# Two of layer 1's adaLN groups made in layer 1's own mixers, with staging of their own

## The chip, the cores and the metric

The kernel runs on one core of a Trainium2 chip. The metric is the device time of one execution in microseconds. The kernel before takes 2099.42 us (median of three runs, 2098.45 to 2099.58).

The core has five engines that run their own instruction lists beside each other: TensorE (PE, matrix products and transposes), VectorE (DVE), ScalarE (ACT), GpSimd (POOL), and SyncE (SP), which here issues all loads. PE writes to PSUM, the others read it from there; everything else lives in the on-chip memory SBUF, and weights come from HBM by DMA.

## The reference, cut to what matters

Two layers, a stream of 256 context tokens and 256 latent tokens, width 1024, float32. In the last layer only the latent tokens are updated. Each layer first needs six modulation vectors (adaLN) for each of two conditions, from one wide product:

```
def adaln_params(cond, lp):
    return jnp.split(jax.nn.silu(cond) @ lp['w_ada'] + lp['b_ada'], 6, axis=-1)

def trunk_layer(xc, xl, c, c_ctx, lp, row, col, update_ctx):
    mod_l = [m[:, None, :] for m in adaln_params(c, lp)]
    mod_c = adaln_params(c_ctx, lp)
    hc = modulate(xc, mod_c[0], mod_c[1])
    hl = modulate(xl, mod_l[0], mod_l[1])
    yc, yl = token_mixer(hc, hl, lp, row, col, update_ctx)
    xl = layer_norm(ALPHA * xl + mod_l[2] * yl, lp['ln1_g'], lp['ln1_b'])
    fl = expert_choice_ffn(modulate(xl, mod_l[3], mod_l[4]), lp)
    xl = layer_norm(ALPHA * xl + mod_l[5] * fl, lp['ln2_g'], lp['ln2_b'])
    ...
```

The token mixer has three branches, an S5 state space, a latent attention (MLA) and a windowed attention. Each branch output is projected (w_branch) and multiplied by a sigmoid gate of 1024 columns; then one output projection (w_out) follows. The feed-forward part has 16 experts (w_gate, w_up, w_down: 3 x 4 MB each). Vectors 0 and 1 are needed before the mixers, 2 to 5 only behind them.

## The kernel before

**Stages.** The program goes through layer 0 and then layer 1. In each: layer norm and modulation, projection to the branches' inputs, the S5 main loop, its GLU, the window projections and the window attention, MLA, output projection and router, experts. In the trace S5's loop stands at 135 to 245 us (layer 0) and 1285 to 1376 (layer 1), the experts at 740 to 1200 and 1660 to 2076.

**The S5 loop** (`s5_main`) has eight steps. Step m records `head(m)` (matmuls into "sc", products L842 and L843 on DVE, sums on POOL, eight scans L852), then `tail(m - 1)` (matmuls into "mm", copies on ACT, transposes into "tp"), the tables of the next head (L818 to L825), `turn(m)` (L862, L863 and POOL's L868), and then a tick.

**Fill work.** A tick adds to a debt in the planner's price unit; while there is debt, `step` takes the next piece of a fill generator (`gates`, `branches`, `gated`) and records it there. One gate is one w_in load of 1024x128 (0.5 MB), its split into two rounded parts (L404 on ACT, L407 on DVE or POOL; "wc"), and 24 matmuls into "F". Every piece of fill work also pays into `ada_debt`, and while that is positive, `step` takes the next step of an adaLN group.

**An adaLN group** (`ada_group`) makes two of the six vectors for both conditions: eight steps (k), each with two loads of w_ada of 128x1024 (0.5 MB) and eight matmul instructions into "ad" (two records each in the trace, `ad<-arena,silu_c`), priced 1.6; then its end: the sum with the bias row on DVE (L376), four transposes into "tp", and copies to modT (L384, L386). Of the six groups (layer, number), (0,0) is made at the start, and the five others are queued in layer 0, before its S5 loop. Their loads take turns in the staging ring "stg" with all w_in and w_branch loads.

**Order on the engines.** The code records instructions; a scheduler then orders each engine's list from the dependencies. A slot of a PSUM tag ("tp" has two, "sc" and "mm" two, "F" and "ad" one) goes from one user to the next in the order in which they were recorded, so a later user can't pass an earlier one of the same tag.

**Late columns.** The last 4096 columns of the on-chip arena (`LATE`) are held by a buffer "late" that no instruction uses during the mixers; they are freed for the experts.

Of the kernel before, what the change touches and what calls it, by code (L numbers as in the profile page):

```python
# [157 lines left out]
class Net:  # L158
# [48 lines left out]
    def step(self):  # L207
        try:
            us = next(self.fillq[0])
            self.debt -= us  # L210
            self.ada_debt += us
        except StopIteration:
            self.fillq.pop(0)
        while self.adaq and self.ada_debt > 0:
            try:
                self.ada_debt -= next(self.adaq[0])
            except StopIteration:
                self.adaq.pop(0)
# [132 lines left out]
    def ada_group(self, l, g, bufs=None):  # L351

        nc = self.nc
        R = self.adarow[(l + g) % 2]
        self.load(R, self.ins["b_rep"][l, g])
        pt = self.ps("ad")
        scv = self.sc.rearrange("p (k s) -> p k s", s=32)
        src = self.ins["w_ada"][l, g]
        for k in range(KT):
            if bufs and k < 7:  # L360
                self.load(bufs[k], src[k])
                ws = [bufs[k][:, 0:1024], bufs[k][:, 1024:2048]]
            else:
                ws = []
                for h in range(2):
                    ws.append(self.stg())
                    self.load(ws[h], src[k, :, 1024 * h:1024 * h + 1024])
            for h in range(2):
                for j in range(4):

                    i = self.mm(pt[32 * j:32 * j + 32, 256 * h:256 * h + 256], scv[:, k, :],
                                ws[h][:, 256 * j:256 * j + 256], k == 0 and h == 0, k == KT - 1)
                    if k == 0 and h + j:
                        self.tc.keep_in_program_order(i)
            yield 1.6
        nc.vector.tensor_tensor(R, pt, R, op=OP.add)  # L376
        tp = self.ps("tp")
        for b in range(4):
            self.tr(tp[:, b * 128:(b + 1) * 128], R[:, b * 128:(b + 1) * 128])
        tv = tp.rearrange("p (b jj jm s) -> p jj jm b s", b=4, jj=2, jm=2)  # L380
        for jj in range(2):
            m = 2 * g + jj
            dst = self.modT[l % 2][:, m].rearrange("p (jm b) s -> p jm b s", jm=2)
            self.nc.vector.tensor_copy(dst, tv[:, jj, :, :, 0:2])  # L384
            if m in (1, 4):
                nc.vector.tensor_scalar(self.modT[l % 2][:, m], self.modT[l % 2][:, m], 1.0, None, op0=OP.add)  # L386
        self.adaR[l % 2, g] = True
        yield 0.0

    def mod_row(self, l, m, s, dst, scale=1.0):  # L390
# [1299 lines left out]
    def build(self, layers=(0, 1), stop=None):  # L1690
        tc, nc = self.tc, self.nc
        self.dbg_out = {}
        self.fillq, self.adaq, self.debt, self.ada_debt = [], [], 0.0, 0.0
        with tc.tile_pool(name="main", bufs=1) as main, \
                tc.tile_pool(name="small", bufs=1) as small, \
                tc.tile_pool(name="ps", bufs=1, space=PSUM) as psum:
            self.small, self.psum, self.main = small, psum, main
            self.sc = main.tile([128, KT * 32], F32, name="silu_c")
            self.modT = [main.tile([128, 6, KT, 2], F32, name=f"modT{i}") for i in range(2)]
            k1 = main.tile([128, 4], F32, name="k1")  # L1700
            self.mhalf, self.econst, self.hpi, self.ones1 = [k1[:, i:i + 1] for i in range(4)]
            for ap, val in ((self.mhalf, -0.5), (self.econst, math.e), (self.hpi, math.pi / 2), (self.ones1, 1.0)):
                nc.vector.memset(ap, val)
            self.const = main.tile([128, NCONST], F32, name="const")
            arena = main.tile([128, self.ARENA_COLS], F32, name="arena")
            self.A = Arena(arena, self.ARENA_COLS)
            self.adaR, self.OH, self.ah, self.cd, self.back, self.norm, self.rw, self.rrow = {}, {}, {}, {}, {}, {}, {}, {}
            self.buf("late", 4096, at=self.LATE)
            self.adarow = [self.buf(f"ada{i}", 512, low=True) for i in range(2)]
            x = {t: self.buf(f"x{t}", D, low=True) for t in range(4)}  # L1710
            self.ada_start()
            self.load(self.const[:, 0:128], self.ins["const"][:, 0:128])
            self.S, self.early, self.stats, self.T, self.feed = {}, [], {}, {}, lambda: None
            self.setup = self.s5_setup(layers[0], self.S, 16)
            next(self.setup)
            self.stg = self.rot("stg", 1024, 4, True)
            hb = [self.block(f"h{i}", F32) for i in range(2)]
            bufs = [hb[i // 2][:, 2048 * (i % 2):2048 * (i % 2) + 2048] for i in range(4)]
            bufs += [self.block(f"extra{i}", F32)[:, 0:2048] for i in range(2)] + [self.buf("wada", 2048, True)]
            for k, _ in enumerate(self.ada_group(layers[0], 0, bufs)):  # L1720
                if k == 4:
                    for t in range(4):
                        self.load(x[t], self.xin(t))
                if k in (7, 8):
                    kc = len(self.early)
                    self.early.append(self.wload(self.w_in(layers[0], 0, 512)[:, 2 * kc:2 * kc + 2], 2, 512))
            self.free("wada")
            for l in layers:
                self.layer(l, x, 1 if l == 0 and 1 in layers else None)
            for t in (2, 3):  # L1730
                self.load(self.out[0, (t - 2) * 128:(t - 1) * 128], x[t])

    def xin(self, t):
        return self.ins["ctx" if t < 2 else "x"][0, (t % 2) * 128:(t % 2) * 128 + 128]

    def layer(self, l, x, nxt):
        tc, nc = self.tc, self.nc
        full = l == 0
        q0 = 0 if full else 256
        N = 512 - q0  # L1740
        with tc.tile_pool(name=f"parts{l}", bufs=1, reuse_waits="tile") as self.R:
            if l:
                self.stg = self.rot("stg", 1024, 3, at=20288)
            step, pts = self.s5_product(l)
            if (l % 2, 1) not in self.adaR:
                self.load(self.const[:, 128:], self.ins["const"][:, 128:])
            h = self.modulated_split(l, x, [full or t < 2 for t in range(4)], step, self.stats)
            self.free(*[f"x{t}" for t in range(4 if full else 2)])
# [2 lines left out]
                pass  # L1751
            S = self.S
            Z = self.proj_tok(l, h, full)
            if (l % 2, 1) not in self.adaR:
                self.adaq += [self.ada_group(l, 1), self.ada_group(l, 2)]
            if nxt is not None:
                self.adaq += [self.ada_group(nxt, g) for g in range(3)]
            mT = self.buf("mT", KT * N, True, 12416 if full else None).rearrange("p (k n) -> p k n", k=KT)
            self.fill(self.gates(l, h, 0, mT, q0))
            if not full:  # L1760
# [78 lines left out]
        with tc.tile_pool(name=f"late{l}", bufs=1, reuse_waits="tile") as pool:  # L1839
            NS = 2 if full else 1  # L1840
            xs = pool.tile([128, 2048 * NS], F32, name="xs")
            XS = xs.rearrange("p (g k e c) -> p g k e c", g=2, k=KT, e=4)
            XS = [XS[:, g] for g in range(2)]
            grow(blocks=[] if full else [(pool.tile([128, 2048], F32, name="more"), 192)],
                 single=[xs[:, 2048:]] if full else [])
            self.free(*[f"m2{s}" for s in m2])
            grow(*T["F2"])
            AFF = self.buf("raff", 64 * NS, at=T["raff"]).rearrange("p (t s e) -> p t s e", t=2, s=NS)
            nc.gpsimd.memset(AFF, 0.0)
            for s in ((1, 0) if full else (1,)):  # L1850
                self.out_norm(l, pts[s], x, s, gb)
                if s == 2 - NS:
                    self.free("lngb")
                    grow(*T["F3"])
                tags = ("sc", "sc", "F", "ad") if NS == 1 or not s else ("tp", "tp")
                self.scores(l, s, x, s + NS - 2, AFF, tags)
            self.free(*[f"x{t}" for t in tts])
            grow(*T["F4"])
            self.choose(l, AFF, NS)
            grow(*T["F5"])  # L1860
            pts = self.moe(l, x, self.xn, full, weight, XS, nxt)
            self.T = {}
            tts = (0, 1, 2, 3) if full else (2, 3)
            self.free(*[n for n in self.A.live if n[0] in "EF"])
            self.buf("late", 4096, at=self.LATE)
            self.finish(l, x, pts, nxt is not None)

    ARENA_COLS = 27456
# [86 lines left out]
```

## Time and profile before

| | |
|---|---|
| median of 3 runs | 2099.42 us |
| the profiled execution | 2097.34 us |
| its span | 2095.6 us |
| PE / DVE / ACT / POOL busy | 86% / 50% / 29% / 22% of the span |
| mean granted TensorE clock | 0.917 |
| read from HBM | 541.09 MB |

The span runs from the first to the last instruction of the trace; the 1.7 us between it and the time of that execution lie outside. A busy share is an average over stages with different limits, so a stage has to be read for itself. A wait is written with what ended it ("<-"). In the chain of waits each piece is the work, transfer or wait that the end of the kernel hangs on at that moment.

### The profile page before, as it was taken

To read this page: it belongs to the slowest core of one execution; us is meant where nothing else is said; L and a number is where in the kernel's file an instruction comes from. 1 tells how busy PE (TensorE), PEld (TensorE's weight loads), DVE (VectorE), ACT (ScalarE), POOL (GpSimd) and SP (SyncE) were. 2 spreads that over 40 slices of the span, in tenths; PEclk is the share of its full clock that TensorE was granted. 3 is DMA by queue.
4 is the path that set the end of the run, shared out by engine and by line. 5 is a ranking of instruction groups with operands and counts; after the bars stand their busy time and mean duration, and the time that the engine had idled before them with its cause. 6 is when DMAs were issued, how large, how long until landed. Compare 5 with 4: busy or idle time off the path is not lost.

```text
span 2095.6 us, 31733 instructions
## 1 busy us (share of the span) xinstructions
PE 1791.9 (86%) x12425; PEld 1112.2 (53%) x12425; DVE 1042.9 (50%) x2431; ACT 611.3 (29%) x1353; POOL 451.5 (22%) x590
## 2 busy tenths in 40 slices
PE   5899899999999699999799979799998776676765
PEld 2876666677777544434233368787786532232221
DVE  6767666756528712313555367977767321010102
ACT  2444253344424311101111165654553110000000
POOL 5735320011125100001343034641114000000000
PEclk8999999999999799999999989999999888776777
DMA  9236744522247689999999733342267799999996
GB/s 334 67 123 218 245 144 163 163 78 71 60 132 274 248 354 421 421 421 416 416 413 351 297 91 94 81 129 63 76 214 297 291 420 421 421 421 421 420 421 272
DMA packets 173013, 544.20 MB, mean 260 GB/s; under 512 B 18624, under 2 KB 101696, under 8 KB 122816
## 3 DMA queue, kind: packets, MB, share of 16 engines
q1 hardware_dynamic: 172864, 542.18, 68.2%
q8 instruction: 98, 1.61, 0.3%
q14 instruction: 51, 0.42, 0.1%
HBM read 541.09 MB, written 1.05 MB: 259 GB/s over the span
## 4 chain that ended last, share of the span: by engine, by line
PE 54%; DMA 23%; DVE 14%; POOL 3%; ACT 3%; issue 3%; SPq 0%; POOLq 0%; ACTq 0%; DVEq 0%
PE sc L243 16%; PE mm L243 16%; PE F L243 13%; DMA arena<-in_w_down 4%; DMA arena<-in_w_up 4%; PE tp L246 4%; PE ad L243 4%; DMA arena<-in_w_gate 3%; DVE extra L852 2%; DVE wc L407 2%; DMA h<-in_w_gate 2%; DMA big<-in_w_gate 2%; DMA arena<-in_w_in 1%; DMA extra<-in_w_up 1%; DMA extra<-in_w_gate 1%
## 5 line engine op out<-in xcount | busy, mean ns | idle before, releaser
L243 PE MATMUL F<-h,wc 128*128 128x256 f32 (+1 forms) x1200 | 237.1, 350 | 11.3 <-ACT arena L1295 9.0
L404 ACT ACTIVATE wc<-arena 128x512 fp32r<-128x512 f32 (+2 forms) x280 | 169.9, 619 | 208.6 <-DMA arena<-in_w_in 45.8
L407 DVE TENSOR_TENSOR wc<-arena,wc 128x512 fp32r<-128x512 f32 (+2 forms) x205 | 163.3, 808 | 112.9 <-ACT wc L404 112.5
L243 PE MATMUL sc<-arena,xs 128*32 128x256 f32 (+1 forms) x1336 | 188.5, 522 | 33.7 <-DMA arena<-in_w_up 20.5
L243 PEld LDWEIGHTS F<-h,wc 128*128 128x128 f32 x1200 | 188.5, 196 | 42.6 <-ACT arena L1295 9.9
L243 PE MATMUL mm<-arena 128*32 128x256 f32 (+5 forms) x1244 | 186.1, 467 | 21.9 <-DMA arena<-in_w_down 13.4
L246 PE MATMUL tp<-const,arena 128*128 128x128 f32 (+2 forms) x819 | 137.5, 293 | 70.4 <-DVE arena L1618 11.6
L1641 DVE TENSOR_TENSOR arena<-mm,arena 32x512 f32<-32x512 f32 (+1 forms) x128 | 70.9, 554 | 219.0 <-PE mm L243 217.4
L407 POOL TENSOR_TENSOR wc<-arena,wc 128x512 fp32r<-128x512 f32 (+2 forms) x75 | 96.9, 1292 | 376.3 <-ACT wc L404 316.7
L246 PEld LDWEIGHTS tp<-const,arena 128*128 128x128 f32 (+2 forms) x819 | 97.3, 147 | 130.5 <-issue 38.5
L238 ACT ACTIVATE arena<-tp 128x512 f32<-128x512 f32 (+3 forms) x142 | 61.9, 463 | 341.7 <-PE tp L246 297.4
L260 POOL TENSOR_TENSOR lnq<-lnq,k 128x1 f32<-128x1 f32 x22 | 16.5, 750 | 568.8 <-DVE lnq L307 530.0
L243 PEld LDWEIGHTS sc<-arena,xs 128*32 128x32 f32 (+1 forms) x1336 | 60.8, 131 | 139.7 <-issue 68.7
L243 PEld LDWEIGHTS mm<-arena 128*32 128x32 f32 (+2 forms) x1244 | 76.3, 137 | 107.2 <-issue 50.5
L243 PE MATMUL sc<-h,xs 128*32 128x256 f32 (+1 forms) x752 | 112.3, 533 | 21.0 <-DMA h<-in_w_gate 13.2
L1618 DVE TENSOR_TENSOR arena<-arena,sc 128x512 f32<-128x512 f32 (+1 forms) x32 | 17.7, 554 | 178.2 <-PE sc L243 177.9
L243 PE MATMUL sc<-big,xs 128*32 128x256 f32 (+1 forms) x632 | 80.8, 487 | 25.2 <-DMA big<-in_w_gate 13.0
L1616 ACT ACTIVATE arena<-sc 128x512 f32<-128x512 f32 (+1 forms) x32 | 15.7, 491 | 295.1 <-PE sc L243 295.1
L243 PE MATMUL mm<-wc,h 128*128 128x512 f32 (+2 forms) x288 | 79.1, 399 | 11.3 <-ACT h L496 4.4
L243 PE MATMUL F<-extra,wc 128*128 128x256 f32 (+1 forms) x432 | 85.7, 343 | 3.5 <-DVE arena L1330 3.1
L1617 DVE SCALAR_TENSOR_TENSOR arena<-arena,sc 128x512 f32<-128x512 f32 (+1 forms) x32 | 17.7, 554 | 142.3 <-ACT arena L1616 142.2
L243 PEld LDWEIGHTS sc<-h,xs 128*32 128x32 f32 (+1 forms) x752 | 36.8, 133 | 89.2 <-issue 60.7
(344 smaller groups left out, 3183.1 us busy)
## 6 DMA issues: line engine op xcount, KB each, us to landing
arena<-in_w_up SPq DMA_DIRECT2D x65, 1024.0 KB, 16.8
arena<-in_w_down SPq DMA_DIRECT2D x61, 1024.0 KB, 19.8
arena<-in_w_gate SPq DMA_DIRECT2D x48, 1024.0 KB, 19.7
arena<-in_w_ada SPq DMA_DIRECT2D x82, 512.0 KB, 5.0
h<-in_w_gate SPq DMA_DIRECT2D x41, 1024.0 KB, 15.0
arena<-in_w_in SPq DMA_DIRECT2D x66, 512.0 KB, 4.0
big<-in_w_up SPq DMA_DIRECT2D x26, 1024.0 KB, 19.8
h<-in_w_down SPq DMA_DIRECT2D x26, 1024.0 KB, 18.6
```

What stands on the lines that cost most here:

```text
L238: self.nc.scalar.activation(out, in_, AF.Copy)
L243: return self.nc.tensor.matmul(out, lhsT, rhs, start=start, stop=stop, skip_group_check=True)
L246: self.nc.tensor.transpose(out, in_, self.c("idn")[:n, :n])
L260: self.nc.gpsimd.tensor_tensor(out, in_, e.to_broadcast(list(in_.shape)), op=OP.pow)
L404: nc.scalar.activation(hi, src, AF.Copy)
L407: eng.tensor_tensor(lo, src, hi.bitcast(F32), op=OP.subtract)
L852: v.tensor_tensor_scan(z, rb, z, 0.0, op0=OP.mult, op1=OP.add)
L1616: nc.scalar.activation(th, gu[0][:, :NF], AF.Tanh, scale=0.5)
L1617: v.scalar_tensor_tensor(th, th, 1.0, gu[0][:, :NF], op0=OP.add, op1=OP.mult)
L1618: v.tensor_tensor(th, th, gu[1][:, :NF], op=OP.mult)
L1641: v.tensor_tensor(YS[n][o:o + 32, c * NF:(c + 1) * NF], yp[r:r + 32, :NF], m5[r:r + 32], op=OP.mult)
```

## The change

In layer 0 the queue holds three groups, (0,1), (0,2) and (1,0); (1,1) and (1,2) are queued in layer 1, before its S5 loop. What a piece of fill work pays into `ada_debt` is multiplied by `ADA`, 0.35 in layer 0 and 0.2 in layer 1. The adaLN loads get a ring of their own (`astg`) in the late columns: four buffers in layer 0, three in layer 1, where the two bias rows (`adarow`) take the rest. The record of finished groups (`adaR`) goes, and two conditions with it.

```
@@ step @@
-            self.ada_debt += us
+            self.ada_debt += us * self.ADA
@@ ada_group @@
-                    ws.append(self.stg())
+                    ws.append(self.astg())
...
-        self.adaR[l % 2, g] = True
@@ build @@
-            self.buf("late", 4096, at=self.LATE)
+            self.take_late(4)
...
+    def take_late(self, n):
+
+        late = self.buf("late", 4096, at=self.LATE)
+        bufs = [late[:, i:i + 1024] for i in range(4096 - 1024 * n, 4096, 1024)]
+        if n < 4:
+            self.adarow = [late[:, 0:512], late[:, 512:1024]]
+        at = [0]
+
+        def nxt():
+            at[0] += 1
+            return bufs[(at[0] - 1) % n]
+
+        self.astg = nxt
@@ layer @@
+        self.ADA = 0.35 if full else 0.2
...
-            if (l % 2, 1) not in self.adaR:
+            if full:
                 self.load(self.const[:, 128:], self.ins["const"][:, 128:])
...
-            if (l % 2, 1) not in self.adaR:
-                self.adaq += [self.ada_group(l, 1), self.ada_group(l, 2)]
+            self.adaq += [self.ada_group(l, 1), self.ada_group(l, 2)]
             if nxt is not None:
-                self.adaq += [self.ada_group(nxt, g) for g in range(3)]
+                self.adaq.append(self.ada_group(nxt, 0))
...
-            self.buf("late", 4096, at=self.LATE)
+            self.take_late(3)
             self.finish(l, x, pts, nxt is not None)
```

The lines of DVE's and PE's lists below are one lower in the changed kernel (L842 is L841 there, L407 is L406), because a line above them went.

VectorE in layer 1's S5 loop, kernel before, from the end of head 3 to head 4; `sc_9387` and `sc_9404` are the two PSUM tiles of head 4, `wc` are weight splits:

```order
L852 SCALAR_TENSOR_TENSOR extra_8866<-s5rho,extra_8866 128x128 x2
L862 TENSOR_TENSOR arena<-extra_8866,arena 128x256
L863 TENSOR_TENSOR arena<-extra_8866 128x256
L852 SCALAR_TENSOR_TENSOR extra_8866<-s5rho,extra_8866 128x128 x2
L407 TENSOR_TENSOR wc<-arena,wc 128x512
L862 TENSOR_TENSOR arena<-extra_8866,arena 128x256
L863 TENSOR_TENSOR arena<-extra_8866 128x256
L842 TENSOR_TENSOR arena<-sc_9387,extra_8866 128x512
L843 TENSOR_TENSOR arena<-sc_9387,extra_8865 128x512
L821 TENSOR_SCALAR arena<-extra_8866 128x516
L822 SCALAR_TENSOR_TENSOR arena<-arena,extra_8866 128x516
L842 TENSOR_TENSOR arena<-sc_9404,extra_8866 128x512
```

The same place in the changed kernel; `ad_8868` is the PSUM tile of group (1,2), `tp_8860` and `tp_8950` hold the transposes of the two groups:

```order
L862 TENSOR_TENSOR arena<-extra_8685 128x256
L406 TENSOR_TENSOR wc<-arena,wc 128x512
L820 TENSOR_SCALAR arena<-extra_8685 128x516
L821 SCALAR_TENSOR_TENSOR arena<-arena,extra_8685 128x516
L384 COPY modT_66<-tp_8860 128x16 x2
L406 TENSOR_TENSOR wc<-arena,wc 128x512 x10
L376 TENSOR_TENSOR arena<-ad_8868,arena 128x512
L406 TENSOR_TENSOR wc<-arena,wc 128x512
L384 COPY modT_66<-tp_8950 128x16 x2
L386 TENSOR_SCALAR modT_66<-modT_66 128x16
L406 TENSOR_TENSOR wc<-arena,wc 128x512 x2
L841 TENSOR_TENSOR arena<-sc_9387,extra_8685 128x512
```

Between heads 3 and 4 stand now the last copies of the first group, the whole end of the second and 14 splits; in the kernel before one split stood there.

TensorE behind head 4 in the kernel before: `mm_9421` and `mm_9422` are the tiles of tail 3, `F_9361` is the seventh gate (G6):

```order
L243 MATMUL sc_9404<-arena,big_7003 64x128 x4
L243 MATMUL mm_9421<-arena,big_7002 64x64
L243 MATMUL mm_9422<-arena,big_7002 64x64
L243 MATMUL mm_9421<-extra_8865,big_7001 64x64
L243 MATMUL mm_9422<-extra_8865,big_7001 64x64
```

and in the changed kernel:

```order
L243 MATMUL sc_9404<-arena,big_6822 64x128 x4
L243 MATMUL F_9361<-h_8242,wc 128x256
L243 MATMUL F_9361<-h_8243,wc 128x256
L243 MATMUL F_9361<-h_8242,wc 128x256 x2
L243 MATMUL F_9361<-h_8243,wc 128x256
L243 MATMUL F_9361<-h_8242,wc 128x256 x2
L246 MATMUL tp_8860<-const,arena 128x128 x4
L243 MATMUL ad_8868<-arena,silu_c 32x256 x8
```

From here on the list holds G6 to G14 (nine gates) and the 64 instructions of `ad_8868` between them, in pieces of 4 or 8; behind them come the transposes `tp_8950`, G15 and the first matmul of tail 2.

SyncE in layer 0, from the loads of the last gates on, kernel before; `in_w_in 128x8x128` is one gate's weights or one of the five loads of the window projections:

```order
L229 DMA arena<-in_w_in 128x8x128
L229 DMA arena<-in_w_ada 128x1024 x3
L229 DMA arena<-in_s_w_glu 128x4x512
L229 DMA arena<-in_w_ada 128x1024 x3
L229 DMA arena<-in_b_rep 128x512
L229 DMA arena<-in_w_in 128x8x128 x5
L229 DMA arena<-in_w_branch 128x4x256
```

and in the changed kernel:

```order
L229 DMA arena<-in_w_in 128x8x128
L229 DMA arena<-in_w_ada 128x1024 x2
L229 DMA arena<-in_w_in 128x8x128
L229 DMA arena<-in_s_w_glu 128x4x512
L229 DMA arena<-in_w_ada 128x1024 x3
L229 DMA arena<-in_w_branch 128x4x256
L229 DMA arena<-in_w_ada 128x1024
```

All 13 loads of w_in stand ahead of s_w_glu now, with two w_ada loads between two of them where there were up to six.

## Rows read from the trace of the kernel before

**Rows 1.** The page's head and busy table: engine, busy us (share), instructions.

```profile
span 2095.6 us, 31733 instructions
PE 1791.9 (86%) x12425; PEld 1112.2 (53%) x12425; DVE 1042.9 (50%) x2431; ACT 611.3 (29%) x1353; POOL 451.5 (22%) x590
```

**Rows 2.** Table by stage: stretch, us, busy of PE, PEld, DVE, ACT, POOL, PEclk, DMA, GB/s.

```profile
130.00:260.00 130.00, 114.92 (x1155) 77.65 (x1154) 96.01 (x162) 48.09 (x92) 64.50 (x75) 0.97 0.65 214
...
300.00:420.00 120.00, 117.65 (x773) 79.49 (x772) 79.68 (x244) 46.62 (x134) 8.75 (x8) 0.99 0.48 156
...
1280.00:1376.00 96.00, 76.61 (x871) 70.73 (x872) 88.99 (x151) 57.09 (x106) 64.05 (x77) 0.93 0.37 96
1376.00:1402.00 26.00, 26.00 (x165) 23.21 (x162) 15.84 (x43) 14.86 (x45) 7.70 (x11) 0.93 0.44 131
...
1660.00:2096.00 436.00, 293.95 (x3104) 119.05 (x3096) 63.12 (x148) 23.36 (x56) 1.10 (x2) 0.76 0.97 402
```

**Rows 3.** Chain of waits in layer 0: start us, us, what.

```profile
183.35 3.00 PE ad L243 x32
...
224.24 5.09 PE F L243 x21
...
231.32 4.88 DMA arena<-in_w_ada
...
236.95 5.67 DMA arena<-in_w_in
...
251.64 5.45 DMA arena<-in_w_in
...
402.23 4.03 DMA arena<-in_w_ukvp
```

**Rows 4.** SyncE's queue, layer 0: start us, us, instruction, count.

```profile
144.65 18.24 SPq L229 DMA_DIRECT2D arena<-in_w_ada  x6
162.99 1.64 SPq L229 DMA_DIRECT2D arena<-in_w_in  x1
...
271.14 3.66 SPq L229 DMA_DIRECT2D arena<-in_w_in  x3
```

**Rows 5.** Table by stretch, of the adaLN matmuls (silu_c) alone; last PE, PEld, DVE.

```profile
100.00:245.00 145.00, 24.00 (x328) 8.87 (x328) 0.00 (x0) 0.98 0.56 185
245.00:300.00 55.00, 7.02 (x88) 2.17 (x88) 0.00 (x0) 1.00 0.62 192
300.00:420.00 120.00, 18.26 (x224) 6.35 (x224) 0.00 (x0) 0.99 0.48 156
```

**Rows 6.** VectorE's timeline, layer 0's S5, first and last head: start us, us, instruction.

```profile
135.49 0.69 DVE L842 TENSOR_TENSOR arena<-sc,extra 128x512 f32<-128x512 f32 x1 [1.67 <-PE sc L243]
...
233.69 0.69 DVE L842 TENSOR_TENSOR arena<-sc,arena 128x512 f32<-128x512 f32 x1 [2.13 <-PE sc L243]
```

**Rows 7.** Costliest groups from 130 to 260 us: instruction, count, busy us, mean ns, idle before.

```profile
L243 PE MATMUL mm<-extra,big 64*64 64x128 f32 x256 | 22.9, 276 | 2.0 <-POOL extra L868 2.0
L243 PE MATMUL sc<-arena,big 64*64 64x128 f32 x256 | 17.6, 272 | 0.0
```

**Rows 8.** Chain of waits in layer 1, S5 and behind it.

```profile
1307.32 3.04 PE F L243 x24
...
1375.43 0.91 PE mm L243 x24
1376.34 4.32 PE F L243 x22
...
1382.48 3.04 PE F L243 x24
...
1387.83 1.77 PE F L243 x15
...
1390.46 1.06 PE F L243 x9
```

**Rows 9.** VectorE's timeline, layer 1's S5.

```profile
1296.80 0.40 DVE L862 TENSOR_TENSOR arena<-extra,arena 128x256 f32<-128x256 f32 x1
1297.11 0.41 DVE L863 TENSOR_TENSOR arena<-extra 128x256 f32<-128x256 f32 x1
...
1305.99 2.44 DVE L852 TENSOR_TENSOR_SCAN extra<-s5rho,extra 128x128 f32<-128x128 f32 x4
1308.35 0.40 DVE L862 TENSOR_TENSOR arena<-extra,extra 128x256 f32<-128x256 f32 x1
...
1324.41 0.69 DVE L842 TENSOR_TENSOR arena<-sc,extra 128x512 f32<-128x512 f32 x1 [0.31 <-issue]
1325.02 0.68 DVE L843 TENSOR_TENSOR arena<-sc,extra 128x512 f32<-128x512 f32 x1
```

**Rows 10.** Table by stretches of 20 us, columns as in rows 2.

```profile
240.00:260.00 20.00, 17.27 (x152) 9.96 (x145) 6.95 (x10) 5.10 (x14) 4.99 (x5) 1.00 0.83 279
1300.00:1320.00 20.00, 17.18 (x194) 16.10 (x194) 18.35 (x32) 12.14 (x24) 15.54 (x17) 0.87 0.33 81
...
1620.00:1640.00 20.00, 8.83 (x67) 7.19 (x67) 14.41 (x51) 7.20 (x16) 2.20 (x4) 0.65 0.58 224
...
1660.00:1680.00 20.00, 20.00 (x362) 11.63 (x358) 4.01 (x11) 3.91 (x6) 0.00 (x0) 1.00 1.01 420
```

More of the change, by code (lines that the diff above doesn't have):

```diff
@@ L1706, in build @@
             self.A = Arena(arena, self.ARENA_COLS)
-            self.adaR, self.OH, self.ah, self.cd, self.back, self.norm, self.rw, self.rrow = {}, {}, {}, {}, {}, {}, {}, {}
-            self.buf("late", 4096, at=self.LATE)
+            self.OH, self.ah, self.cd, self.back, self.norm, self.rw, self.rrow = {}, {}, {}, {}, {}, {}, {}
+            self.take_late(4)
             self.adarow = [self.buf(f"ada{i}", 512, low=True) for i in range(2)]
```

## The prediction

> **What bounds the kernel now.** The page's head and busy table come first: TensorE (PE) is busy for 86% of the span, VectorE (DVE) for 50% [rows 1]. Those shares are averages, so the second view is the table by stage [rows 2]. The reader is to see four things in it. From 300 to 420 us PE is busy 117.65 of 120: what PE is spared there comes back as time. From 130 to 260 (layer 0's S5 and what follows) PE has 114.92 of 130 and DVE 96.01: neither is full, and the chain of waits must say who is late. From 1280 to 1376 (layer 1's S5) DVE has 88.99 of 96, PE 76.61: DVE bounds it. From 1660 on the transfers are busy 97% of the time at 402 GB/s: layer 1's experts cost what their bytes cost, and mixers that end later by some time end the kernel later by that time.
>
> Third, the chain through layer 0 [rows 3]. It holds 3.00 us of adaLN matmuls (PE ad, x32), a wait of 4.88 us for a transfer of w_ada, and two for w_in, 5.67 and 5.45 us. The sync queue shows why w_in is late [rows 4]: a single load stands behind six of w_ada (18.24 us for one such six), all through one staging ring, and the first loads of the window projections go out only at 271.14. A last wait, 4.03 us at 402, is for w_ukvp [rows 3]. So the adaLN groups hurt layer 0 today.
>
> **Part 1, what layer 0 is spared.** Two of five groups leave it. The adaLN matmuls by themselves [rows 5] take 24.00 + 7.02 + 18.26 = 49.28 us of PE for 328 + 88 + 224 = 640 records, five groups: 9.9 us each, two are 19.7.
>
> Inside S5: the DVE work of the first of its eight heads begins at 135.49, that of the last at 233.69 [rows 6], so seven steps take 98.2 us, 14.0 each. In PE's order a step has about one gate (24 matmuls; at 5.09 for 21 [rows 3] 5.8 us), one head and one tail (17.6 and 22.9 us over eight, side by side in part [rows 7]: some 4 us) and until now 20 to 24 adaLN instructions (9.9 us over 64, so 3.4): 13.2 together, near the step of now. With 8 such instructions left PE needs 11, and DVE's 96.01/8 = 12.0 at most [rows 2] becomes the limit. I take 1.5 us a step, -11 in all, between -5 (the POOL and ACT waits inside the steps stay) and -14.
>
> Behind S5: w_in no longer queues behind w_ada (sync order in the change section). Of the 5.67 and 5.45 us I take -7, between -3 and -11, because about as many adaLN instructions stay behind S5 as stood there before. The load of w_ukvp now stands ahead of most of w_ada: -3, between 0 and -4. The own staging adds no instruction and no byte. The loads that move before 60 us I cost at nothing, 2 us either way: POOL and DVE carry that stretch. Layer 0: **-21 us**, between -8 and -28.
>
> **Part 2, what layer 1 gets.** "A fifth of the rate" isn't what the code does. The debt that releases adaLN steps is never cleared. Layer 0's fill work is priced by the planner at 40.8 (gates) + 20.8 (branches) + 2 x 61.6 (gated) = 184.8; times 0.35 that is 64.7, and three groups at 8 x 1.6 use up 38.4. So 26.3 are left when layer 1 begins, and its two groups cost 25.6: both are recorded whole at the first tick of S5, behind head 0. (These are the planner's prices, not times.) The transposes' two PSUM slots go out in recorded order, so the groups' ends come ahead of the transposes of every S5 tail.
>
> What this does stands in the orders of the change section. DVE has four heads, then ten weight splits, the end of the second group, three splits, and only then head 4. On PE nine gates and all 64 instructions of the second group follow head 4, and tail 2 comes after them. So S5, which DVE bounds, stands still for that run: 9 x 3.04 us a gate [rows 8] + 9.9 + about 1 for transposes and copies = 38. The run starts when PE has the sixth gate behind it, some 8 us after head 4's DVE work begins now (1324.41 [rows 9]; one more gate, and a part of the first group that DVE doesn't hide), so that work begins at 1333 + 38 = 1371. The four heads left are then almost pure DVE work: 16 products x 0.605 + 32 scans x 0.57 + 16 smaller products x 0.335 + 5.3 for tables and splits = 38.6 (from start to start in [rows 9]), with a tenth of waits 42.5; now they take 1376 - 1324.4 = 51.6. S5 ends at about 1414: **+38**.
>
> Given back: the gates that fill the stretch behind S5 are done by then. Of its 26 us (1376 to 1402) gates on the chain are 4.32 + 3.04 + 1.77 + 1.06 = 10.2 [rows 8]: -10, between -4 and -16. Splits of window weights that DVE has done earlier: -2.
>
> The run's weights: nine gates' w_in and 16 halves of w_ada, 25 x 0.5 = 12.5 MB, of which six buffers (3 MB) can be there before. The trace doesn't show this mix beside S5. The other 9.5 MB take 23 us at the 420 GB/s of the expert stage, 72 at the 131 of 1376 to 1402 (when little was asked for), and 34 at the 279 of 240 to 260, where the same two kinds of loads alternate [rows 2, 10]. I take the last: hidden under 38, though narrowly.
>
> While DVE works alone, PE has only tails and heads left. With PE busy 8.83 of 20 us the granted clock is 0.65, near the lower level of 1.2 GHz; with 17.18 of 20 it is 0.87 [rows 10]. The first matmuls behind S5 pay for that: +1, between 0 and +3. Layer 1: 38 - 10 - 2 + 1 = **+27**, between +10 (the ends hold DVE for half the run only) and +36 (the low end of what is given back, and the run 3 longer).
>
> By the Trainium skill (TensorE: Matmul & The Clock Gate, Part 1, "What's actually happening") an array that has gone idle falls to 1.2 GHz, which speaks against emptying a stretch of its filling work. The four tails there, 0.91 us each on the chain [rows 8], would double: by that rule the sum would be some 4 us more. By the row the tails stay beside a busy DVE (14.41 of 20 at clock 0.65), and the sum stands.
>
> **The sum.** -21 + 27 = +6; I take +5, a little nearer to no change, since both terms are large and are worked out alike. The profiled execution took 2097.34 us (span 2095.6), 2.1 under the median of 2099.42. So 2102 for such an execution and 2104 against the median.
>
> **Rivals.**
> 1. Layer 0's gain decides. PE is so full there that all 19.7 us and most of the waits come back (-28), and in layer 1 the run costs +13, because DVE gets half of head 4 done before it and the glu finds everything ready. For it: 117.65 of 120. Against it: DVE's queue stands behind the group's end. 2099.4 - 15 = 2084. The sign turns, with -21 in layer 0, where S5 in layer 1 ends less than 32 us later within its layer (32 - 12 + 1 = 21).
> 2. The work only changes places: 19.7 us of PE out of layer 0, 19.7 into layer 1, no more: 2099. For it: the sum of instructions is the same. Against it: in layer 1 PE isn't what bounds.
> 3. The run is starved: one sync queue issues w_ada and w_in in turn, so one full ring holds up both. At 200 GB/s the 9.5 MB take 47 us, the run is 10 longer (+37), and layer 0 gives only 16: 2120. For it: the 4.88 and 5.67 us waits on these very loads. Against it: separate rings now.
> 4. The groups are spread as the words say, and my reading of the debt is wrong. Then 19.7 us of PE go in small pieces into S5 and the gates, where PE has 19.4 idle: +5 in layer 1, -21 in layer 0, 2083. Against it: the recorded order.
>
> **How the numbers follow.** 0.2% (4.2 us) is about what a measurement of this kernel can tell from no change. The forecast (S5 in layer 1 stands still, layer 0 gives some 20) has a chance of 0.5, on its own from 2097 to 2113. Rival 1 has 0.2, rival 2 0.14, rival 3 0.12, rival 4 0.04. Faster: rivals 1 and 4 and a rest of the forecast, 0.28. Slower: two thirds of the forecast, rival 3, a rest of rival 2: 0.49. Within: 0.23. The range from 2086 to 2122 leaves out rival 4 and about half of rival 1, and the worst of rival 3.
>
> **What would show it.** Right: in layer 1's S5 DVE has over 20 us idle or in splits between head 3 and head 4, at the end of an adaLN group, while PE runs gates back to back; layer 0's expert stage begins some 20 us earlier. Wrong: it begins less than 10 us earlier (part 1 is oversized), or layer 1's S5, counted from that layer's start, ends less than 20 us later (part 2 is). If PE's waits for w_ada in layer 1 pass 8 us in all, rival 3 holds.

## The result and the profile after

The changed kernel takes 2117.83 us (median of four runs, 2115.32 to 2119.61) against 2099.5 for the kernel before in the same rounds: a ratio of 1.0085, interval 1.0068 to 1.0103. It is slower by 18 us, where +5 was forecast. The head of its page:

```profile
span 2116.9 us, 31701 instructions
PE 1806.6 (85%) x12425; PEld 1120.2 (53%) x12425; DVE 1035.2 (49%) x2431; ACT 606.8 (29%) x1349; POOL 445.0 (21%) x590
```

The engines run about as many instructions as before [rows 1], PE the same 12425. PE is busy 14.7 us longer with them; DVE, ACT and POOL are busy for less. Where the 21.3 us lie by which the span grew shows when the same instructions of both kernels are set side by side (starts in us from the span's start, read from VectorE's timeline; the product of S5's heads is L842 before and L841 after, the line of the layer's residual sum L1386 and L1385; shifts are of the unrounded starts):

| | before | after | shift |
|---|---|---|---|
| last head's product in layer 0's S5 | 234.9 | 229.9 | -5.0 |
| MLA's first step in layer 0 | 434.9 | 419.1 | -15.8 |
| first head's product in layer 1's S5 | 1272.8 | 1259.3 | -13.5 |
| last head's product in layer 1's S5 | 1365.8 | 1398.7 | +33.0 |
| residual sum behind layer 1's out_proj | 1624.5 | 1646.1 | +21.7 |
| end of the span | 2095.6 | 2116.9 | +21.3 |

So layer 0 gives 13.5 us, layer 1's S5 takes 46.5 more, the stages behind it give 11.3 back, and the experts pass on what they get. Layer 1's S5 in the table by stage, columns as in [rows 2]:

```profile
1266.00:1362.00 96.00, 86.57 (x839) 67.13 (x836) 51.57 (x90) 44.09 (x72) 37.13 (x41) 0.93 0.82 258
1362.00:1390.00 28.00, 22.88 (x280) 18.60 (x280) 22.88 (x45) 9.79 (x29) 16.03 (x24) 0.89 0.35 96
1646.00:2082.00 436.00, 299.97 (x3209) 128.77 (x3211) 70.67 (x189) 27.56 (x62) 1.65 (x3) 0.76 0.98 404
```

Over the 96 us in which VectorE was 88.99 us busy before [rows 2] it is busy for 51.57 now: the engine that bounds the stage stands still nearly half of the time. Its timeline says at which instruction (start, us, instruction, idle time before it and what ended that):

```profile
1309.73 0.68 DVE L841 TENSOR_TENSOR arena<-sc,arena 128x512 f32<-128x512 f32 x1
...
1317.78 0.67 DVE L376 TENSOR_TENSOR arena<-ad,arena 128x512 f32<-128x512 f32 x1
...
1324.90 0.69 DVE L406 TENSOR_TENSOR wc<-arena,wc 128x512 fp32r<-128x512 f32 x1 [2.91 <-ACT wc L403]
1330.86 0.69 DVE L406 TENSOR_TENSOR wc<-arena,wc 128x512 fp32r<-128x512 f32 x1 [5.27 <-ACT wc L403]
...
1359.41 0.69 DVE L376 TENSOR_TENSOR arena<-ad,arena 128x512 f32<-128x512 f32 x1 [1.39 <-PE ad L243]
...
1362.86 0.26 DVE L384 COPY modT<-tp 128x16 f32<-128x16 f32 x2 [2.16 <-PE tp L246]
...
1368.49 0.69 DVE L841 TENSOR_TENSOR arena<-sc,extra 128x512 f32<-128x512 f32 x1 [2.55 <-POOL extra L867]
```

Between head 3 (1309.73) and head 4 (1368.49) lie the ends of both groups and 14 splits, as the order had them. In the kernel before the two heads are 12.1 us apart (1312.35 and 1324.41), here 58.8. The line of head 3 there (that of head 4 stands in [rows 9]):

```profile
1312.35 0.69 DVE L842 TENSOR_TENSOR arena<-sc,arena 128x512 f32<-128x512 f32 x1 [0.76 <-POOL extra L868]
```

The chain of waits through that stretch:

```profile
1318.50 0.66 PE tp L246 x4
1319.16 1.00 PE ad L243 x16
...
1327.23 5.28 PE F L243 x23
...
1334.10 7.22 DMA arena<-in_w_ada
...
1359.34 3.04 PE F L243 x24
1362.39 0.66 PE tp L246 x6
1363.04 2.80 PE F L243 x23
1366.55 1.32 PE mm L243 x36
```

Gates, adaLN and one transfer of w_ada follow one another until the second group's transposes are done; only then comes the first tail (mm, 1366.55). The transfers of 1320 to 1365, packets first, then issues with their size and median us to landing:

```profile
DMA packets 11387, 12.25 MB, mean 272 GB/s; under 512 B 366, under 2 KB 9554, under 8 KB 11383
...
arena<-in_w_ada SPq DMA_DIRECT2D x13, 512.0 KB, 6.5
arena<-in_w_in SPq DMA_DIRECT2D x10, 512.0 KB, 6.9
```

Of the 16 loads for the second group 13 are issued in this stretch, the three before them by 1315.4; the 12.25 MB also hold loads for what stands behind the run (ln_b, ln_g and the last of w_in). PE's waits in the run, from 1318.5 to the first tail (what waited, us in total, times, longest), and behind the dots the row for the whole of layer 1's S5 (1265 to 1400):

```profile
PE ad L243 <- DMA arena<-in_w_ada: 3.0, 2, 2.2
PE F L243 <- ACT arena L1294: 1.3, 1, 1.3
...
PE ad L243 <- DMA arena<-in_w_ada: 4.6, 5, 2.2
```

The adaLN matmuls alone, by stretch, columns as in [rows 5]:

```profile
100.00:245.00 145.00, 8.36 (x128) 3.44 (x128) 0.00 (x0) 0.92 0.37 108
245.00:300.00 55.00, 8.07 (x104) 3.40 (x104) 0.00 (x0) 1.00 0.51 167
300.00:420.00 120.00, 13.53 (x152) 4.81 (x152) 0.00 (x0) 1.00 0.37 117
1255.00:1320.00 65.00, 11.17 (x144) 3.18 (x144) 0.00 (x0) 0.95 0.71 217
1320.00:1365.00 45.00, 8.97 (x116) 2.35 (x112) 0.00 (x0) 0.92 0.87 272
```

Layer 0 has 29.96 us of them instead of 49.28 [rows 5]; layer 1 has 20.1. Layer 0's queue is what the order promised: two w_ada loads stand between two of w_in, and from 125 to 420 us PE waits for a load only once, 1.0 us for w_ada.

```profile
182.94 0.80 SPq L229 DMA_DIRECT2D arena<-in_w_ada  x2
189.84 0.38 SPq L229 DMA_DIRECT2D arena<-in_w_in  x1
```

### The profile page after: what moved, and what is told of

It reads as the page before. It is cut to its first block, busy times and chain, and to the rows that moved or that the text cites. A ratio compares the mean times of both kernels' runs of the same rounds, so it can differ in the third digit from the quotient of the medians.

```text
span 2116.9 us, 31701 instructions
## 1 busy us (share of the span) xinstructions
PE 1806.6 (85%) x12425; PEld 1120.2 (53%) x12425; DVE 1035.2 (49%) x2431; ACT 606.8 (29%) x1349; POOL 445.0 (21%) x590
## 4 chain that ended last, share of the span: by engine, by line
PE 55%; DMA 22%; DVE 16%; ACT 3%; issue 3%; POOL 2%; SPq 0%; POOLq 0%; ACTq 0%; DVEq 0%
PE sc L243 17%; PE mm L243 16%; PE F L243 13%; PE ad L243 4%; PE tp L246 4%; DMA arena<-in_w_down 4%; DMA arena<-in_w_up 4%; DMA arena<-in_w_gate 3%; DVE extra L851 3%; DVE wc L406 2%; DVE arena L549 2%; DMA big<-in_w_gate 2%; DMA h<-in_w_gate 2%; DMA extra<-in_w_up 1%; DMA arena<-in_w_out 1%
## 5 line engine op out<-in xcount | busy, mean ns | idle before, releaser
L406 DVE TENSOR_TENSOR wc<-arena,wc 128x512 fp32r<-128x512 f32 (+2 forms) x205 | 161.1, 798 | 117.7 <-ACT wc L403 116.5
L246 PE MATMUL tp<-const,arena 128*128 128x128 f32 (+2 forms) x819 | 137.9, 292 | 66.0 <-DVE arena L1617 11.1
L406 POOL TENSOR_TENSOR wc<-arena,wc 128x512 fp32r<-128x512 f32 (+2 forms) x75 | 96.5, 1286 | 445.2 <-ACT wc L403 356.4
L243 PE MATMUL mm<-wc,h 128*128 128x512 f32 (+2 forms) x288 | 78.7, 397 | 15.8 <-DVE h L503 7.6
## 6 DMA issues: line engine op xcount, KB each, us to landing
h<-in_w_gate SPq DMA_DIRECT2D x41, 1024.0 KB, 13.3
```

What stands on the lines that cost most here:

```text
L243: return self.nc.tensor.matmul(out, lhsT, rhs, start=start, stop=stop, skip_group_check=True)
L246: self.nc.tensor.transpose(out, in_, self.c("idn")[:n, :n])
L406: eng.tensor_tensor(lo, src, hi.bitcast(F32), op=OP.subtract)
```

## The experiments

Two theories were set against each other. The wall: the loss comes from the ends of both groups being recorded ahead of S5's tails, so that DVE stands still behind them. The load: 19.7 us of PE work and 16 MB cost layer 1's mixers some 35 us wherever they are put. For all kernels, from their traces (us; the first to the last head's L842 product is "S5"; "between" is from there to the residual sum; ratios are to the kernel before in the same rounds, with their intervals). Each trace is one execution. The seven kernels with the same layer 0 (after, e1, e2, e7, e9, e10, e11) begin layer 1's S5 between 1256.5 and 1260.9, so some 4 us in that column are differences between executions:

| kernel | S5 of layer 1 begins | S5 | between | median | ratio |
|---|---|---|---|---|---|
| before | 1272.8 | 93.0 | 258.7 | | 1 |
| after | 1259.3 | 139.5 | 247.4 | 2117.83 | 1.0085 [1.0068, 1.0103] |
| e1_clear_debt | 1260.1 | 100.4 | 274.6 | 2106.02 | 1.0023 [1.0012, 1.0034] |
| e2_ad_slot | 1256.5 | 105.9 | 257.2 | 2092.59 | 0.9959 [0.9944, 0.9974] |
| e3_own_staging | 1278.9 | 93.0 | 259.9 | 2103.86 | 1.0014 [1.0004, 1.0024] |
| e5_ad_slot_both | 1264.7 | 105.2 | 260.0 | 2098.94 | 0.9995 [0.9984, 1.0006] |
| e6_shared_l0 | 1262.6 | 105.3 | 256.8 | 2099.56 | 1.0002 [0.9984, 1.0019] |
| e7_two_loads | 1259.3 | 107.2 | 255.1 | 2093.87 | 0.9976 [0.9964, 0.9989] |
| e8_one_in_l1 | 1275.7 | 99.1 | 256.3 | 2103.77 | 1.0028 [1.0014, 1.0042] |
| e9_cleared_ad_065 | 1257.5 | 106.7 | 252.7 | 2090.75 | 0.9950 [0.9931, 0.9968] |
| e10_cleared_ad_02 | 1257.3 | 100.3 | 276.7 | 2107.29 | 1.0027 [1.0014, 1.0041] |
| e11_cleared_tp_065 | 1260.9 | 112.0 | 254.1 | 2098.89 | 0.9991 [0.9975, 1.0006] |

From the residual sum to the last instruction of PE, DVE or ACT all twelve need 464.5 to 468.8 us: what the mixers gain or lose arrives whole.

**Another PSUM tag for the ends (e2_ad_slot).** One word of the changed kernel:

```
         nc.vector.tensor_tensor(R, pt, R, op=OP.add)
-        tp = self.ps("tp")
+        tp = self.ps("ad" if l and g else "tp")
```

> Only the PSUM tag of the four transposes at the end of groups (1,1) and (1,2) is changed, from tp to ad; recording, rates, staging and loads stay as in the changed kernel. By the order the scheduler then puts the groups behind S5's last gates, into the GLU, window and MLA stages. Wall: S5 in layer 1 as long as in the kernel before (within 3 us), layer 1 +10 to +20 in all because the window stage has PE busy for 72 of 78 us, time 2096 to 2108. Load: 2112 to 2119.

The place was read wrongly: the trace has both groups inside S5, in small pieces (the adaLN matmuls from 1255 to 1365, columns as in [rows 5]):

```profile
1255.00:1365.00 110.00, 20.06 (x256) 5.49 (x256) 0.00 (x0) 0.97 0.73 230
```

That makes it the sharper test, since the work, the loads and the stage are those of the changed kernel, and only the tails no longer queue behind the ends, nor behind the gates that those carried along. S5 takes 105.9 us instead of 139.5, the kernel 25 us less than the changed one. VectorE at the first group's end:

```profile
1306.44 0.68 DVE L841 TENSOR_TENSOR arena<-sc,arena 128x512 f32<-128x512 f32 x1
...
1313.58 0.66 DVE L376 TENSOR_TENSOR arena<-ad,arena 128x512 f32<-128x512 f32 x1
...
1316.24 0.85 DVE L406 TENSOR_TENSOR wc<-arena,wc 128x512 fp32r<-128x512 f32 x1
1317.01 0.68 DVE L841 TENSOR_TENSOR arena<-sc,extra 128x512 f32<-128x512 f32 x1
```

Head 4 begins 10.6 us behind head 3 (their first products are at 1306.44 and 1317.01), where it was 58.8. The wall stands; the load theory, which wanted 2112 or more, falls.

**The same for all later groups (e5_ad_slot_both).** `self.ps("ad")` in both layers.

> The transposes at the end of every later group take tag ad instead of tp. By the order layer 1's two groups then stand wholly inside S5, in pieces of 4 between its gates, heads and tails, and no run of gates is left: the same work and loads at about the same place as in the changed kernel, without the wall. Wall: S5 in layer 1 is 4 to 14 us longer than in the kernel before (PE 76.6 + 19.7 of 96 us), time 2088 to 2102. Load or starved transfers (same 16 MB of w_ada in S5): S5 +30 us or more and over 2108.

S5 +12.2 and 2098.94, as the wall has it. Against e2 it loses 8 us in layer 0, 5.8 of them before S5 begins there (140.7 and 134.9); why the tag costs there wasn't followed up (the edit takes in group (0,0), which is made ahead of S5, and this profiled execution is 3.4 us above its kernel's median).

**Clearing the debt (e1_clear_debt).** `self.ada_debt = 0.0` behind the line that sets ADA.

> Sets the adaLN debt to zero when layer 1 begins, so that a fifth of the fill work's price releases its groups. By the order no group ends inside layer 1's S5: five k-steps stand between its gates, the rest behind it. Theory of the wall (the recorded ends of both groups hold up every later S5 tail, DVE stands still): S5 in layer 1 is at most 8 us longer than in the kernel before, layer 1 pays 8 to 16 us for the 19.7 us of PE work, time 2092 to 2104. Theory of the load (19.7 us of PE and 16 MB cost about 35 us wherever they are put in layer 1's mixers): 2112 to 2119, as the changed kernel.

S5 is 7.4 us longer, as the wall says, but the time is 2 us above its range. The loss has moved: "between" is 274.6 instead of 258.7. The adaLN matmuls there:

```profile
1255.00:1365.00 110.00, 7.16 (x66) 2.13 (x66) 0.00 (x0) 0.92 0.45 129
1365.00:1400.00 35.00, 5.74 (x70) 1.84 (x70) 0.00 (x0) 0.95 0.75 242
1400.00:1480.00 80.00, 10.39 (x120) 3.24 (x120) 0.00 (x0) 0.98 0.43 145
```

Three quarters of the records now fall behind S5, where PE is full (71.82 of 78 us before, in the stretch from 1402). At the rate that its words name, the change would have lost too.

**The rate of 0.2 with the ends on "ad" (e10_cleared_ad_02).**

> Layer 1's group ends on tag ad, the debt cleared, and the rate of 0.2 as written: about half of the work falls behind S5. Clearing alone, with the ends on tp, gave 2106. If the place is what costs there (GLU and window stages with PE full): 2102 to 2108 again. If it was the ends that hold the tp slots of the window stage: 2090 to 2098.

2107.29: the place costs, not the slots of the window stage.

**The rate that fits (e9_cleared_ad_065 and e11_cleared_tp_065).** The debt cleared and `0.65` instead of `0.2`; e9 has the ends on "ad", e11 leaves them on "tp".

> Layer 1's group ends on tag ad, the debt cleared at layer 1's start, and a rate of 0.65, at which its two groups (25.6) fit into the fill work of S5 (16 gates at 2.55 are 40.8): nearly the same as the ad slot by itself, but spread to the last gates instead of ahead of them. Wall: no tail waits, S5 8 to 13 us longer than in the kernel before; if what S5 pays comes from the group that crowds its first steps (5.3 us of DVE waiting for PE ahead of head 2), 2 to 5 us better than the ad slot alone: 2087 to 2092. If it comes from PE's sum over S5 (76.6 + 20 of 96 us): the same, 2091 to 2096.

> The changed kernel with two numbers alone: the debt cleared when layer 1 begins and a rate of 0.65 there; the group ends stay on tag tp. Recorded in pace with S5's steps, they hold up only tails that are recorded after them. Wall (recorded too early is the fault, not the tag): 2088 to 2096, as the same pace with tag ad. If the ends on tp hold up S5's tails wherever they are recorded: 2100 or more.

e9 is the best of all, 0.9950, but its interval overlaps with e2's: whether the crowded first steps cost S5 anything is not told apart. e11 lies between its two expectations. Recording in pace takes away most of the wall (S5 112.0, not 139.5), but not all: with the ends on "tp" S5 is 5.3 us longer than in e9. Another 3.4 us of the difference between the two profiled executions lie ahead of layer 1's S5, where both kernels are alike, so they belong to the runs.

**The loads left out (e7_two_loads).** Weights are loaded for k = 0 only.

> The changed kernel with the weights of each of layer 1's two groups loaded for the first k-step only and used for all eight (7/8 of these 16 MB aren't loaded, the vectors are not the reference's); the ends stay on tag tp, recorded at the first tick. By the order both groups then stand as one block behind gate 0, and no run of gates is left. Wall (what counts is how long the S5 tails wait for the ends, and loads in a ring of three spread that): S5 in layer 1 is 12 to 22 us longer than in the kernel before instead of 46, time 2092 to 2104. If the 19.7 us of PE work or the tp slots by themselves made the loss: over 2110.

S5 is 14.2 us longer, 2093.87, inside the expectation. Both groups stand between heads 1 and 2 (1272.12 and 1303.43 in this trace), as two blocks of 128 records with 15.86 us of PE in all; heads 3 and 4 are 11.1 us apart, with no run of gates between them. So a wall is there too, but a short one: the ends' place makes it, and in the changed kernel the loads of three buffers spread the second group over nine gates and make it long. PE's own waiting for these loads is the smaller part of that, 3.0 us of the 48.

**Own staging by itself (e3_own_staging).** All five groups in layer 0, ADA = 1, own ring.

> All five groups stay in layer 0 at the old rate; only the own staging in the late columns is kept. Layer 1 must read as in the kernel before. For layer 0's gain of 13.5 us at layer 1's start: if it is the queue (w_in no longer behind w_ada), 5 to 10 us come back, time 2089 to 2095; if it is the PE work that left, under 3 us, 2096 to 2101.

Neither: the kernel takes 2103.86, and in its trace layer 1 begins 6.1 us later than before (that execution is 2.6 us above its kernel's median, the one of the kernel before 2.1 below; the ratio says 0.8 to 5 us). The adaLN matmuls take more of PE than before and come earlier:

```profile
120.00:250.00 130.00, 26.25 (x352) 9.25 (x352) 0.00 (x0) 0.97 0.62 206
250.00:300.00 50.00, 8.82 (x78) 2.50 (x78) 0.00 (x0) 1.00 0.55 186
300.00:420.00 120.00, 20.86 (x210) 7.07 (x210) 0.00 (x0) 0.96 0.44 142
```

55.93 us for the same 640 records, 49.28 before.

**Shared staging in layer 0 (e6_shared_l0)**, e2 with `stg` for layer 0's w_ada.

> As the kernel with the ad slot for layer 1's two group ends (2092.6 us), but layer 0's w_ada loads take turns in the shared staging ring again; the own ring serves layer 1 alone. If the own staging is what cost the 6 us that layer 0 lost when it was put in by itself, layer 1 begins 19 to 22 us earlier than in the kernel before instead of 16, time 2085 to 2090. If it helps once only three groups are left in layer 0 (the queue theory of the prediction: w_in behind w_ada), time 2095 to 2101.

The other way round: layer 1 begins 6 us later than in e2, and the kernel takes 7 us more. With three groups left, the shared ring delays them so far that the last one falls into MLA, and w_in waits behind it again:

```profile
420.00:640.00 220.00, 12.87 (x128) 3.87 (x128) 0.00 (x0) 1.00 0.42 131
```

```profile
461.23 5.80 DMA arena<-in_w_in
...
470.36 5.00 DMA arena<-in_w_ada
```

MLA began 26.0 us earlier than before (434.9 to 408.9) and kept 7.3 of it to layer 0's residual sum (691.8 to 684.5).

**One group in layer 1 (e8_one_in_l1)**, e6 with (1,1) in layer 0.

> As the kernel with shared staging in layer 0, but only group (1,2) is made in layer 1, (1,1) stays in layer 0. If each group costs 9.9 us of PE in layer 0 and about half of that in layer 1's S5, where PE has idle time: 3 to 6 us slower than with both in layer 1, 2089 to 2096. If S5 in layer 1 takes one group for nothing and pays for the second alone: no slower than with both, 2083 to 2089.

S5 takes 99.1 with one group and 105.3 with two, 93.0 with none: about 6 us each, not the first for nothing. The kernel is 4.2 us slower than e6, as the first case has it, though the two intervals overlap a little; its level is that of e6, off for e6's reason.

## Why the prediction was right, and where it wasn't

The mechanism is the one that was forecast, and shown: the debt that isn't cleared, both groups recorded at the first tick, DVE's queue behind their ends. Between heads 3 and 4 DVE waits 30.3 us for ACT's halves of the splits, where over 20 us idle or in splits were named as the sign. The direction was right, and 2117.8 lies in the range, but the predicted 2104 is 14 us short. Both terms were off, to the same side.

**Part 1, -21: it was -13.5.** The step that failed is S5's, "1.5 us a step, -11": from the first head to the last it came to -5.4 (135.70 to 228.49, 92.8 us instead of 98.2). PE's list got as short as was worked out: PE is busy for 78.41 of the 92.8 us, 11.2 a step. DVE is busy for 11.8 a step, but a step takes 13.3, where 14.0 had been and 12.5 was foreseen, because waits stay: 5.6 us ahead of L820 for POOL's tables, 3.7 for ACT's halves of the splits. The longest two:

```profile
188.61 1.48 DVE L820 TENSOR_SCALAR arena<-arena 128x516 f32<-128x516 f32 x1 [2.31 <-POOL arena L817]
...
203.62 0.43 DVE L820 TENSOR_SCALAR arena<-extra 128x516 f32<-128x516 f32 x1 [2.31 <-POOL extra L817]
```

That was the term's lower bound. The stretch behind S5 gave 10.8 by MLA's beginning, where -7 and -3 were named. But the reason was half of it: e3 shows that with five groups the own staging gives nothing and costs some 3.5 us by the medians, e2 and e6 that it is worth some 7 once three groups are left. Why the ring costs with five groups stays open; the adaLN matmuls hold PE for 6.6 us more there, and PE once waits 4.6 us for a group's sum (L376), where its longest such wait was 1.9 before. 2.3 us went again on the way through layer 0, whose residual sum comes 14.0 us earlier (691.8 to 677.8), not "some 20".

**Part 2, S5 +38: it was +46.5.** The place was right and the length wasn't. The run was to begin at 1333 of the kernel before; it begins with the first group's transposes at 1318.50, which is 1332.0 there, since the layer begins 13.5 us earlier. So the delay of the heads before it (head 3 begins 10.9 us later within its layer) was allowed for. But it was put at 38 us of PE work, and from there to the first tail (1366.55) it took 48. The whole run and three short stretches in it, columns as in [rows 2]:

```profile
1318.50:1366.55 48.05, 43.74 (x378) 34.91 (x379) 12.49 (x24) 19.22 (x37) 9.14 (x7) 0.93 0.84 261
...
1324.00:1328.00 4.00, 1.41 (x11) 0.93 (x12) 0.69 (x1) 3.67 (x6) 0.22 (x1) 0.73 0.96 381
1328.00:1332.00 4.00, 4.00 (x21) 4.00 (x20) 0.69 (x1) 0.63 (x1) 1.05 (x1) 0.50 0.60 167
...
1360.00:1364.00 4.00, 4.00 (x36) 3.92 (x35) 1.73 (x6) 2.07 (x7) 1.28 (x1) 1.00 0.86 227
```

The term that was too small is "9 x 3.04 us a gate + 9.9 + about 1". It lacks a tenth gate: the order has G15 ahead of tail 2 as well, 2.80 us on the chain (1363.04). It lacks PE's waits, 4.3 us, 3.0 of them for w_ada. And it takes every gate at the full clock: behind the first two waits, where PE was busy for 1.41 of 4 us, the granted clock is 0.50, the level of 1.2 GHz, and the 23 matmuls at 1327.23 take 5.28 us on the chain, where the 23 at 1363.04, at 1.00, take 2.80. That is 2.5 us more. Together these are 9.6 of the 10 us; that no other delay hides under them isn't shown.

"Hidden under 38, though narrowly" came close: the rate was near the chosen one (272 GB/s, 279 chosen), three w_ada loads were out ahead of the run, and PE stood still for the others for 3.0 us. The 7.22 us of w_ada on the chain are a transfer beside which PE worked on; PE waited 0.85 us at its end. Head 4 was to begin 46.6 us later; it is 57.6 (1324.41 to 1368.49, and the 13.5). The four heads behind it went as foreseen: from head 4 to the last product 30.2 us instead of 41.3, 11 less, where 9 was worked out.

**Given back, -12 and +1: it was -11.3.** The gates were done, as forecast. TensorE's clock fell while DVE caught up (columns as in [rows 2]); in the 20 us before, PE was busy for 15.86 and the clock was 0.95:

```profile
1386.00:1406.00 20.00, 13.05 (x131) 9.81 (x132) 19.56 (x40) 5.42 (x18) 12.34 (x20) 0.59 0.24 80
```

The granted clock of 0.59 is near the level of 1.2 GHz, though PE was busy for 13.05 of the 20 us. By the Trainium skill (TensorE: Matmul & The Clock Gate, Part 1, "What's actually happening") the clock follows how busy the array has been, and the trace agrees: 0.95 at 15.86 of 20 us, 0.59 at 13.05. DVE was busy for 19.56 of the 20, so PE was not what S5 waited for there, and the 4 us that the rule would have added aren't seen; the +1 can't be told from the rest. The clock cost more where the prediction had put nothing, in the run.

**The rivals.** Rival 3 (the run starved, 2120) has the nearest number, and for the larger part by luck: the run is 10 us longer, as it says, but PE's waits for w_ada are 3.0 us of that, and 4.6 in all of layer 1's S5, where its own mark was 8. Rival 4's number for a spread that works, 2083, is too low: spread groups cost layer 1 8 to 14 us (e2, e5, e9), not 5, and spread at the rate as written they cost 23 to 25. Rivals 1 and 2 are out by the wall: layer 1 lost 35.2 us in all (46.5 less 11.3), not 13 and not 19.7.

## What to carry to other kernels

Where slots of a pool are handed out in recorded order, the recorded place of a short tail (here a sum, four transposes, two copies) can hold up a loop far more than the work ahead of it: give such a tail a slot that the loop doesn't use, or record it when its inputs will be there. A rate that is meant to spread work doesn't act as long as a credit from an earlier stage isn't cleared; and once it is, the rate decides in which stage the work falls, and each stage has its own price for it (layer 1's S5 about 6 us for 10 us of PE work, the full stages behind it 16 to 18 us for the 16 us that fell there in e1 and e10). To size a stretch of one engine's list, count all that stands in it up to the instruction that the others wait for, here a tenth gate, and leave room for waits inside it and for the slower clock behind them.

## What the runs showed of the hardware

The same 640 records of 128x256 adaLN matmuls held PE for 49.28 us in the kernel before and 55.93 in e3, where they stand in smaller pieces between others. A 0.5 MB load of w_ada landed after 5.0 us (median) in the kernel before and after 6.5 in the run, where 12.25 MB went at 272 GB/s. In the run 23 gate matmuls of 128x256 took 5.28 us where the granted clock was 0.73 and then 0.50, and 2.80 us where it was 1.00.
